# Products of two activations in whole fp32 instead of three products of split parts, in a kernel of two transformer blocks

## The chip, the cores and the metric

One core of a Trainium2 chip runs the whole kernel in one launch. The metric is the device time of an execution in microseconds (us); three executions took 1322.33, 1323.85 and 1326.26 us, the median is 1323.85. The execution that the profiler recorded took 1332.18 us, of which its span (first to last instruction) is 1330.4.

## The reference

Two blocks on 256 tokens of width 1024, all fp32. The first block: a mixer (gated causal convolution of 31 taps beside attention with 8 heads of 64 and a forget gate), attention of 4 heads of 128 over 256 memory rows, and an MLP with squared ReLU of width 4096. The second block puts 16 meta tokens ahead and runs a state space mixer (24 heads of 64 in 4 groups, state 128, chunks of 128 tokens) beside a short convolution, and then a layer of 16384 single-neuron experts:

```
q = (t @ w_q).reshape(T, 8, 2, 128)
s = einsum('thsd,hskd->thsk', q, sub_keys)          # scores against 2 x 128 sub keys
v_half, i_half = top_k(s, 16)                       # then the best 16 of 16 x 16 sums
experts = i1 * 128 + i2                             # 8 x 16 experts a token
act = gelu(einsum('td,tkd->tk', t, expert_u[experts])) * gates
out = einsum('tk,tkd->td', act, expert_v[experts])
```

A final norm gives the output (256 tokens without the meta tokens). The products of two activations are q with k, probabilities with v, the same two against the memory, in the state space mixer C with B, B with x, C with the state and the masked C-B scores with x; the sub key scores are a product of queries with a weight, but its two operands are treated in the same way.

## The kernel before, in words

Tokens lie in two tiles of 128. A weight comes from HBM in units of 128 x 1024 words, two units a transfer, on SyncE's queue. fp32 accuracy in matmuls is kept by splitting: ScalarE rounds an operand to fp32r (`hi`), VectorE or GpSimd subtracts to get the residual (`lo`), and `mm3` (L783) adds three products of fp32r parts, hi hi, hi lo and lo hi, into one PSUM bank. `unit` (L679) loads and splits a weight unit, `split` (L774) splits an activation that stands in PSUM or SBUF, `feat` (L821) multiplies a split weight with split activations (8 blocks of 128 rows, features on the partitions), `tok_unit` and `proj_out` do it with tokens on the partitions.

The products of two activations stand in `attend` (L1097: logits of two heads at a time, softmax, transposes, product with v), `recall` and `recalled` (L1247, L1261: the same against the memory), and in the loop over the four groups of the state space mixer (blocks bc, xt, state and y): B, C, x times dt, the decayed x, the states and the decay matrices times scores (`M`) are each split; `y` multiplies six heads with `M` hi against both halves of x (128 columns) and `M` lo against x hi (64 columns).

The expert layer: `to_n2` (L1603) normalizes, transposes and splits a token tile into `n2T`. `scores` (L1680) makes, for one head, two halves of queries (`feat` on `n2T` with split units of `w_q`), splits them, and multiplies them with split sub keys. Head 0 is done for one token tile at a time, so that its first routing can begin early; `route` is VectorE's top-16 search and index arithmetic. Its indices feed the indirect DMAs of GpSimd: 256 gathers (2 token tiles x 8 heads x 16), each bringing for 128 tokens a row of 2048 words (`expert_u` and `expert_v`), 1.049 MB. VectorE takes the dot product with the first half, ScalarE the GELU, and TensorE adds the second half into two banks, by diag(act) times 512 columns in whole fp32. Heads 1 to 7 have their scores made in the course of the first four heads' gathers. Ten units of `w_q` are loaded ahead into free k2 and act tiles (HELD), the rest come through raw tiles.

SBUF is given out in classes: k8 (tiles of 2048 words, 11 of them: at most 5 for `mid`, 2 `raw`, 4 split weights `w`, 2 split query weights `wq`, 10 gathered rows), act, k4 (1024 words, 4), k3, k2 and k1. PSUM has 2 banks `mm` and 6 `s`.

The order of the work is written by a planner (`Plan`): every operation is recorded with a cost and the tiles it uses, and a list scheduler gives each engine one fixed order; `SHIFTS` move the priority of each named block, `LATERS` say when GpSimd may take an operation that VectorE could do (`q.either`). On the chip each engine follows its list.

Of the kernel before, what the change touches and what calls it, by code (L numbers as in the profile page):

```python
# [33 lines left out]
QCONV = 2  # L34
MID, ROW = 5, 10
# [45 lines left out]
    "attend21.te": 199, "mo.gp": 1828, "state3.ve": -2216, "ln.gp": -447, "dt.sy": -536, "dt.sc": 1092,  # L81
# [107 lines left out]
SPAN = 3413.3  # L189
PIECE = 256  # L190
EARLY = {'s_kp': 3}
WINDOW = 3850
FIRST_MEM = 40
LEAD = 120
# [399 lines left out]
def trace(q, pool, psum, x, mem, meta, wts, sk, uv, cols, gains, ssdn, heads, out):  # L594
# [84 lines left out]
    def unit(k, w=UNIT, lead=None, at=None, place="k4"):  # L679
# [17 lines left out]
        if not lead:  # L697
            q.wait = q.place
# [72 lines left out]
    def sl(pr, *idx):  # L771
        return (pr[0][idx], pr[1][idx])
# [1141 lines left out]
```

## Time and profile before

| | |
|---|---|
| median of three executions | 1323.85 us (1322.33 to 1326.26) |
| profiled execution | 1332.18 us, span 1330.4 us, mean granted TensorE clock 0.975 |
| TensorE busy | 1142.5 us (86%), 5292 matmuls |
| VectorE busy | 956.9 us (72%) |
| ScalarE busy | 576.5 us (43%) |
| GpSimd busy | 494.0 us (37%) |
| DMA by GpSimd's queue | 268.45 MB, 48.8% of the 16 engines' span |
| DMA by SyncE's queue | 108.63 MB, 22.6% |

Every operation is issued by one helper, so the line is L548 throughout and groups are told apart by tiles: `k` stands for any tile of the k classes, `s` and `mm` for the PSUM banks, `s_...` for small tiles. A TensorE row counts instructions; a matmul in whole fp32 is two of them, one on fp32r parts is one. Mean times of matmuls hold the tail of the pipeline. In the slices of the page a digit is the busy share in tenths of a 40th of the span.

### The profile page before, as it was taken

Reading aid. Unit: us, or ns where it says so; the run is one execution under the profiler, and the core shown is the slowest. Engines: PE = TensorE matmul, PEld = TensorE weight load, DVE = VectorE, ACT = ScalarE, POOL = GpSimd, SP = SyncE. Lnnn points to the kernel's source line nnn. Section 1 sums busy time; section 2 is a strip of 40 time slices with the busy share of each in tenths; the row PEclk is TensorE's granted clock in tenths of the full one; section 3 lists DMA queues with packets and bytes.
Section 4 is the critical chain, followed back from the end, with each engine's and each line's share of the span. In section 5 each row is a group of like instructions: output and inputs, shape, how many; then the busy total and the mean of one; then the engine's idle time right before and its main releaser. Section 6 shows DMA issues by size and latency. Waiting matters only on the chain.

```text
span 1330.4 us, 16001 instructions
## 1 busy us (share of the span) xinstructions
PE 1142.5 (86%) x5292; PEld 788.3 (59%) x5292; DVE 956.9 (72%) x2210; ACT 576.5 (43%) x1162; POOL 494.0 (37%) x542
## 2 busy tenths in 40 slices
PE   6999889999998999999999997777778768777776
PEld 5988677999877998888865553332233223223222
DVE  7898877456557897885789999997555555555555
ACT  6647565445445965654354444323122122211221
POOL 4861250300001766431034464543434334343330
PEclk9999988999998999999999999999999999999998
DMA  7433333354554242446599999999999999999995
GB/s 278 150 119 139 146 120 134 128 221 159 197 217 158 100 150 107 161 157 224 190 344 409 410 421 422 421 421 421 422 420 422 421 421 422 421 421 422 422 421 208
DMA packets 55702, 378.09 MB, mean 284 GB/s; under 512 B 6322, under 2 KB 6962, under 8 KB 11460
## 3 DMA queue, kind: packets, MB, share of 16 engines
q0 software_dynamic: 36864, 268.45, 48.8%
q1 hardware_dynamic: 18756, 108.63, 22.6%
q8 instruction: 42, 0.69, 0.2%
q14 instruction: 40, 0.33, 0.1%
HBM read 376.01 MB, written 1.05 MB: 283 GB/s over the span
## 4 chain that ended last, share of the span: by engine, by line
PE 39%; DMA 34%; DVE 15%; issue 5%; ACT 3%; POOL 3%; another core or an unknown queue 0%; SPq 0%; POOLq 0%; DVEq 0%; ACTq 0%
DMA k<-in_uv,s_ei 32%; PE s L548 22%; PE mm L548 17%; DVE k L548 11%; ACT k L548 3%; DMA k<-in_wts 2%; POOL k L548 2%; DVE s_ix L548 1%; DVE s_v L548 1%; POOL act L548 1%; DMA k<-in_ssdn 1%; DMA x<-in_x 1%; DVE s_pos L548 0%; ACT L548 0%; DVE act L548 0%
## 5 line engine op out<-in xcount | busy, mean ns | idle before, releaser
L548 PE MATMUL s<-k,s_dg 128*128 128x512 f32 x1020 | 477.5, 614 | 129.1 <-ACT s_dg L548 128.6
L548 DVE SCALAR_TENSOR_TENSOR k<-k,k 128x1024 bf16<-128x1024 f32 x256 | 313.0, 1223 | 159.5 <-DMA k<-in_uv,s_ei 159.0
L548 PEld LDWEIGHTS s<-k,s_dg 128*128 128x128 f32 x1020 | 187.9, 193 | 400.3 <-ACT s_dg L548 206.6
L548 POOL DMA_INDIRECT k<-in_uv,s_ei x256 | 275.1, 1075 | 380.7 <-PE s L548 227.9
L548 PE MATMUL mm<-act,k 128*128 128x256 f32 (+4 forms) x2448 | 334.9, 289 | 9.0 <-DVE k L548 6.4
L548 PEld LDWEIGHTS mm<-act,k 128*128 128x128 f32 x2448 | 312.8, 191 | 25.0 <-DVE k L548 7.3
L548 ACT ACTIVATE k<-k 128x1024 fp32r<-128x1024 f32 (+11 forms) x293 | 231.3, 823 | 134.6 <-DVE k L548 58.1
L548 DVE TENSOR_TENSOR k<-k,k 128x1024 fp32r<-128x1024 f32 (+11 forms) x239 | 225.0, 970 | 51.7 <-ACT k L548 50.2
L548 POOL TENSOR_TENSOR k<-k,k 128x256 fp32r<-128x256 f32 (+2 forms) x205 | 160.7, 822 | 116.4 <-ACT k L548 100.2
L548 PE MATMUL s<-k,k 128*128 128x512 f32 (+8 forms) x868 | 191.5, 363 | 7.2 <-DVE k L548 3.6
L548 ACT ACTIVATE s_act<-s_dots,rx 128x2 f32<-128x2 f32 x129 | 38.1, 295 | 342.8 <-DVE k L548 342.7
L548 PEld LDWEIGHTS s<-k,k 128*128 128x128 f32 (+2 forms) x868 | 145.9, 191 | 37.2 <-ACT k L548 6.4
L548 ACT ACTIVATE s_dg<-ident,s_act 128x128 f32<-128x128 f32 x255 | 90.6, 394 | 87.4 <-DVE s_act L548 58.9
L548 PE MATMUL s<-k,act 128*128 128x512 f32 (+1 forms) x432 | 103.6, 385 | 1.8 <-ACT act L548 1.3
L548 PEld LDWEIGHTS s<-k,act 128*128 128x128 f32 x432 | 79.6, 194 | 13.8 <-ACT act L548 1.5
L548 ACT ACTIVATE k<-s 128x512 f32<-128x512 f32 (+10 forms) x99 | 46.9, 485 | 56.0 <-PE s L548 39.3
L548 ACT ACT_TABLE_LOAD x52 | 66.7, 1283 | 4.8 <-DVE k L548 2.1
L548 PE MATMUL s<-ident,k 128*128 128x128 f32 (+2 forms) x220 | 39.7, 308 | 30.0 <-DVE k L548 26.4
L548 DVE TENSOR_TENSOR k<-s,k 128x256 f32<-128x256 f32 (+8 forms) x100 | 44.8, 476 | 24.7 <-ACT k L548 15.2
L548 POOL TENSOR_TENSOR s_rstd<-s_ms,nhalf 128x1 f32<-128x1 f32 (+1 forms) x15 | 16.1, 1071 | 115.9 <-DVE s_ms L548 115.6
L548 POOL TENSOR_TENSOR s_r<-s_ms,nhalf 128x1 f32<-128x1 f32 x10 | 7.3, 732 | 127.4 <-DVE s_ms L548 124.0
L548 ACT ACTIVATE k<-mm 128x256 f32<-128x256 f32 (+3 forms) x70 | 25.9, 372 | 60.9 <-PE mm L548 53.3
(174 smaller groups left out, 776.5 us busy)
## 6 DMA issues: line engine op xcount, KB each, us to landing
k<-in_wts SPq DMA_DIRECT2D x89, 1024.0 KB, 4.8
k<-in_gains SPq DMA_DIRECT2D x9, 512.0 KB, 6.4
k<-in_uv,s_ei POOLq DMA_INDIRECT x256, 17.6
k<-in_wts SPq DMA_DIRECT2D x12, 256.0 KB, 7.0
act<-in_wts SPq DMA_DIRECT2D x4, 512.0 KB, 9.4
x<-in_x SPq DMA_DIRECT2D x2, 512.0 KB, 6.8
k<-in_mem SPq DMA_DIRECT2D x2, 512.0 KB, 6.1
k<-in_sk SPq DMA_DIRECT2D x2, 512.0 KB, 6.1
```

The source lines that it names most:

```text
L548: getattr(getattr(self.nc, e), method)(*a, **kw)
```

## The change

Products of two activations, the query projection and the sub key scores take whole fp32 operands, one product each. What made and held the split parts goes; query weights are used as they were loaded (`raw_unit`); `n2T` is one tile, copied half by ScalarE, half by VectorE. k8 has 12 tiles and up to 11 rows, the classes k3, `wq` and `s_kp` go, q and k of the attention share one k8 tile, as do the memory's keys and values, and v, the probabilities of the second token tile and the memory's q move to single k4 tiles. All values of `SHIFTS` and `LATERS` are others (left out here, as are repeated edits).

```diff
-QCONV = 2
-MID, ROW = 5, 10
+N8, MID, ROW = 12, 5, 11
-EARLY = {'s_kp': 3}
+EARLY = {}
...
+    def raw_unit():
+
+        q.shift -= QAHEAD
+        ts = loaded()
+        q.shift += QAHEAD
+        return [t[:, c:c + P] for t in ts for c in range(0, t.ap[-1][1], P)]
...
-            split(dst[0][:, c], dst[1][:, c], ps, scale=scale)
+            q.scalar.activation(dst[:, c], ps, AF.Copy, scale=scale)
...
-                mm3(ps[:, j], sl(qT, b, c0 + j, slice(i * P, i * P + P)),
-                    sl(kT, b, c0 + j, slice(0, kl)), False, j == 1)
+                q.tensor.matmul(ps[:, j], qT[b, c0 + j, i * P:i * P + P], kT[b, c0 + j, :kl],
+                                start=False, stop=j == 1)
...
-            split(PT[0][:, :, :, par], PT[1][:, :, :, par], tp)
+            q.scalar.activation(PT[:, :, :, par], tp, AF.Copy)
...
-            split(xdt[i][:, :, 0], xdt[i][:, :, 1], h6(t), eng=q.either)
+            q.vector.tensor_mul(h6(xdt[i]), h6(ps), hbc(dt3[:, 1 + i, hs]))
...
-        mm3(s1, sl(Bt, A_, 1), xdec, True, True)
+        q.tensor.matmul(s1, Bt[:, 1], xdec, start=True, stop=True)
...
-            M = pair(k4, 6, P)
-            split(M[0], M[1], E[i], eng=q.either)
...
-            mm3(yo, sl(CT, A_, slice(i * P, i * P + P)), pv[i], True, True)
+            q.tensor.matmul(yo, CT[:, i * P:i * P + P], pv[i], start=True, stop=True)
...
-            for h0, n in ((0, 4), (4, 2)):
-                yd = s_bank()[:, :n * P].rearrange("p (h j d) -> p h j d", h=n, j=2)
-                for h in range(n):
-                    q.tensor.matmul(yd[:, h], M[0][:, h0 + h], xdt[i][:, h0 + h], start=True, stop=False)
-                    q.tensor.matmul(yd[:, h, 0], M[1][:, h0 + h], xdt[i][:, h0 + h, 0], start=False, stop=True)
-                for j in range(2):
-                    to = h6(t)[:, h0:h0 + n]
-                    q.vector.tensor_add(to, yd[:, :, j], to)
+            yd = s_bank()[:, :GW]
+            for h in range(6):
+                q.tensor.matmul(h6(yd)[:, h], E[i][:, h], h6(xdt[i])[:, h], start=True, stop=True)
+            q.vector.tensor_add(t, yd, t)
...
-    n2T = pair(act, KD, T)
+    n2T = act(KD, T, dt=F32)
...
-        transposed(n2T, n2[i], i * P, P)
+        for c in range(0, KD, 4):
+            v = s_bank().rearrange("p (c t) -> p c t", c=4)
+            for j in range(4):
+                q.tensor.transpose(v[:, j], n2[i][:, (c + j) * P:(c + j + 1) * P], ident)
+            if c:
+                q.vector.tensor_copy(n2T[:, c:c + 4, i * P:i * P + P], v)
+            else:
+                q.scalar.activation(n2T[:, c:c + 4, i * P:i * P + P], v, AF.Copy)
...
-        kp = []
-        for c in (2 * h, 2 * h + 1):
-            kp.append(pair(lambda n, dt: small(n, "kp", dt), P))
-            split(kp[-1][0], kp[-1][1], skt[c // 8][:, c % 8])
...
-                ws[half] = ws.get(half) or unit(8, lead=0 if whole else None)
-                ps = feat(n2T, i0 * P, n * P, ws[half])
-                qp = pair(k1, n * P)
-                split(qp[0], qp[1], ps)
+                ws[half] = ws.get(half) or raw_unit()
+                ps = mm_bank()[:, :n * P]
+                for k in range(KD):
+                    q.tensor.matmul(ps, ws[half][k], n2T[:, k, i0 * P:(i0 + n) * P], start=k == 0, stop=k == KD - 1)
+                qp = k1(n * P)
+                q.scalar.activation(qp, ps, AF.Copy)
+                c = 2 * h + half
                 for i in range(i0, i0 + n):
-                    mm3(sp_[:, i, half], sl(qp, A_, slice((i - i0) * P, (i - i0) * P + P)),
-                        kp[half], True, True)
+                    q.tensor.matmul(sp_[:, i, half], qp[:, (i - i0) * P:(i - i0) * P + P], skt[c // 8][:, c % 8],
+                                    start=True, stop=True)
```

## Rows read from the trace of the kernel before

**Rows 1.** The page: busy tenths of TensorE and the DMA engines, 40 slices.
```profile
PE   6999889999998999999999997777778768777776
...
DMA  7433333354554242446599999999999999999995
```

**Rows 2.** Busy time by stage: stretch, us, busy (instructions), clock, DMA.
```profile
740.00:1310.00 570.00, 441.37 (x1044) 184.99 (x1043) 382.06 (x1020) 158.39 (x408) 243.02 (x228) 0.98 1.01 421
...
416.00:620.00 204.00, 196.31 (x1304) 181.92 (x1303) 169.72 (x321) 135.23 (x222) 103.32 (x130) 0.98 0.41 145
220.00:400.00 180.00, 178.45 (x1107) 158.93 (x1105) 101.63 (x141) 89.96 (x143) 14.43 (x19) 1.00 0.50 182
```

**Rows 3.** Busy time in slices of 5 us after the first gather.
```profile
665.00:670.00 5.00, 4.60 (x39) 4.39 (x38) 4.25 (x16) 2.63 (x6) 3.78 (x5) 1.00 0.82 282
...
685.00:690.00 5.00, 5.00 (x18) 2.55 (x18) 5.00 (x21) 4.21 (x9) 1.57 (x2) 1.00 0.66 218
...
735.00:740.00 5.00, 5.00 (x24) 3.28 (x23) 5.00 (x26) 2.20 (x5) 2.12 (x2) 1.00 0.96 351
```

**Rows 4.** Timeline of GpSimd, first gathers: start, us, what, [idle before, releaser].
```profile
663.95 1.17 POOL L548 DMA_INDIRECT k<-in_uv,s_ei  x1 [20.29 <-DVE s_gr L548]
...
670.61 1.20 POOL L548 DMA_INDIRECT k<-in_uv,s_ei  x1 [0.30 <-issue]
...
682.46 0.94 POOL L548 DMA_INDIRECT k<-in_uv,s_ei  x1 [6.70 <-PE mm L548]
687.68 1.08 POOL L548 DMA_INDIRECT k<-in_uv,s_ei  x1 [4.29 <-PE s L548]
```

**Rows 5.** Timeline of all engines from the last projection to the first gather.
```profile
639.70 1.28 DVE L548 TENSOR_TENSOR act<-s,act 128x512 fp32r<-128x512 f32 x2
...
644.88 3.11 PE L548 MATMUL mm<-act,k 128*128 128x128 f32 x24
...
648.04 0.28 DVE L548 TENSOR_TENSOR k<-mm,k 128x128 fp32r<-128x128 f32 x1
...
656.66 2.48 DVE L548 TENSOR_TENSOR k<-k,k 128x512 fp32r<-128x512 f32 x4
...
661.29 0.68 DVE L548 TENSOR_TENSOR k<-k,k 128x512 fp32r<-128x512 f32 x1
...
661.89 0.42 DVE L548 TENSOR_TENSOR k<-mm,k 128x256 fp32r<-128x256 f32 x1
662.22 0.68 DVE L548 TENSOR_TENSOR k<-k,k 128x512 fp32r<-128x512 f32 x1
```

**Rows 6.** Timeline of TensorE, 676 to 702 us, dense runs.
```profile
682.93 1.64 PE L548 MATMUL mm<-act,k 128*128 128x256 f32 x12
...
689.37 7.13 PE L548 MATMUL s<-k,s_dg 128*128 128x512 f32 x16
```

**Rows 7.** Timeline of TensorE, 120 to 140 us, dense runs.
```profile
125.50 1.03 PE L548 MATMUL s<-k,inv 128*128 128x256 f32 x4
...
129.78 1.39 PE L548 MATMUL s<-inv,k 128*128 128x1 f32 x12
...
133.81 3.96 PE L548 MATMUL s<-k,k 128*128 128x512 f32 x16
```

**Rows 8.** Groups of TensorE by form, 416 to 620 us.
```profile
L548 PE MATMUL mm<-act,k 128*128 128x272 f32 x367 | 55.4, 293 | 0.6 <-DVE k L548 0.6
...
L548 PE MATMUL s<-a,trilr 16*16 16x24 f32 x2 | 0.2, 184 | 0.0
```

**Rows 9.** Groups of VectorE by form, 416 to 620 us.
```profile
L548 DVE TENSOR_TENSOR k<-k,k 128x384 fp32r<-128x384 f32 x12 | 8.0, 693 | 0.5 <-ACT k L548 0.5
...
L548 DVE TENSOR_TENSOR k<-k,k 128x768 fp32r<-128x768 f32 x6 | 6.1, 1036 | 0.0
```

**Rows 10.** Groups of ScalarE by form, 416 to 620 us.
```profile
L548 ACT ACTIVATE k<-k 128x384 fp32r<-128x384 f32 x20 | 10.0, 521 | 7.0 <-DVE k L548 5.5 <-PE s L548 1.4
```

**Rows 11.** Chain of waits after the first gather: start, us, what.
```profile
708.86 9.24 DMA k<-in_uv,s_ei
```

More of the change, by code (lines that the diff above doesn't have):

```diff
@@ L53 @@
 SHIFTS = {
[27 rows of a table removed]
-    "attend21.te": 199, "mo.gp": 1828, "state3.ve": -2216, "ln.gp": -447, "dt.sy": -536, "dt.sc": 1092,
[83 rows of a table removed]
-LATERS = {
[22 rows of a table removed]
[23 rows of a table added]
+    "mo.gp": 1535, "state3.ve": -1696, "ln.gp": -529, "dt.sy": -251, "dt.sc": 1399, "gate11.sc": -1087,
[84 rows of a table added]
+LATERS = {
[22 rows of a table added]
 SPAN = 3413.3
 PIECE = 256
-EARLY = {'s_kp': 3}
+EARLY = {}
 WINDOW = 3850
@@ L611, in cls @@
         return t.rearrange(pat, **dict(zip(names[:-1], dims[:-1])))
-    N8 = MID + RAW_BUFS + CONV_BUFS
     def k4(*dims, dt=F32):
@@ L677, in load_early, with loaded @@
         q.wait = None
+    def loaded(at=None):
+        if early:
+            return early.pop(0)
+        u = st["next"] if at is None else at
+        st["next"] += at is None
+        if u % 2:
+            return [second_half.pop(u)]
+        t = k8("raw", RAW_BUFS)
+        q.sync.dma_start(t, wts[u // 2])
+        second_half[u + 1] = t[:, UNIT:]
+        return [t[:, :UNIT]]
+    def raw_unit():
[3 more added lines that the diff above has]
+        return [t[:, c:c + P] for t in ts for c in range(0, t.ap[-1][1], P)]
     def unit(k, w=UNIT, lead=None, at=None, place="k4"):
-        ahead = AHEAD if lead is None else QAHEAD
+        ahead = AHEAD
         lead = LEAD if lead is None else lead
         q.shift -= ahead
-        if early:
-            ts = early.pop(0)
-        else:
-            u = st["next"] if at is None else at
-            if u % 2 == 0:
-                t = k8("raw", RAW_BUFS)
-                q.sync.dma_start(t, wts[u // 2])
-                second_half[u + 1] = t[:, UNIT:]
-                ts = [t[:, :UNIT]]
-            else:
-                ts = [second_half.pop(u)]
-            st["next"] += at is None
+        ts = loaded(at)
         q.shift += ahead - lead
-        if not lead:
-            q.wait = q.place
         if place == "k2":
@@ L705, in unit @@
             else:
-                kind = ("wq", QCONV) if not lead else ("w", CONV_BUFS)
-                hi, lo = halves(k8(*kind, F32R), UNIT)
+                hi, lo = halves(k8("w", CONV_BUFS, F32R), UNIT)
             n = UNIT // len(ts)
@@ L713, in unit @@
             q.scalar.activation(h, t, AF.Copy)
-            (q.either if lead else q.vector).tensor_sub(l, t, h.bitcast(F32))
-        q.wait = None
+            q.either.tensor_sub(l, t, h.bitcast(F32))
         q.shift += lead
@@ L1006, in gated @@
         q.vector.tensor_mul(ups[c][:, 30:], ap, sg)
-    qT = pair(k4, 4, T)
-    kT = pair(k4, 4, T)
+    qT, kT = two(4, T)
     def qk(c):
-        for dst, scale in ((qT, 0.125), (kT, None)):
+        for dst, scale in ((qT, 0.125), (kT, 1.0)):
             ps = feat(hT, 0, T)
-            split(dst[0][:, c], dst[1][:, c], ps, scale=scale)
+            q.scalar.activation(dst[:, c], ps, AF.Copy, scale=scale)
     q.block("gated0")
@@ L1083, in trace @@
     q.block("v")
-    vt = pair(k4, NT, 512)
+    vt = k4(NT, 512)
     vp = [s_bank() for i in range(NT)]
@@ L1088, in trace @@
     for i in range(NT):
-        split(vt[0][:, i], vt[1][:, i], vp[i])
+        q.scalar.activation(vt[:, i], vp[i], AF.Copy)
     q.block("qk2")
@@ L1100, in attend @@
         kl = nk * P
-        PT = pair(k4 if i else k2, nk, 2, 2, P)
+        PT = (k4 if i else k2)(nk, 2, 2, P)
         for par in range(2):
@@ L1126, in attend @@
             for k in range(nk):
-                mm3(ps[:, j], sl(vt, A_, k, slice(c * P, c * P + P)), sl(PT, A_, k, j),
-                    k == 0, k == nk - 1)
+                q.tensor.matmul(ps[:, j], vt[:, k, c * P:c * P + P], PT[:, k, j],
+                                start=k == 0, stop=k == nk - 1)
         for b in range(2):
@@ L1169, in trace @@
     q.block("mem")
-    mk = pair(k4, 4, T)
+    mk, mv = two(4, T)
+    mv = mv.rearrange("p a b -> p (a b)").rearrange("p (i n) -> p i n", i=NT)
     mT = pair(act, KD, T)
@@ L1233, in trace @@
         ps = feat(mT, 0, T)
-        split(mk[0][:, c], mk[1][:, c], ps)
+        q.scalar.activation(mk[:, c], ps, AF.Copy)
     q.wait = q.last()
@@ L1243, in trace @@
     q.wait = None
-    qT = pair(k4, 4, T)
+    qT = k4(4, T)
     moT = pair(k4, 4, T)
@@ L1250, in recall @@
         for i in range(NT):
-            mm3(ps[:, i], sl(qT, A_, h, slice(i * P, i * P + P)), sl(mk, A_, h), True, True)
+            q.tensor.matmul(ps[:, i], qT[:, h, i * P:i * P + P], mk[:, h], start=True, stop=True)
         e = softmax(ps, NT, T, scale=rsc)
@@ L1256, in recall @@
                 q.tensor.transpose(tp[:, k, i * P:i * P + P], e[:, i, k * P:(k + 1) * P], ident)
-        PT = pair(k2, 2, T)
-        split(PT[0], PT[1], tp)
+        PT = k2(2, T)
+        q.scalar.activation(PT, tp, AF.Copy)
         return PT
@@ L1263, in recalled @@
         for k in range(2):
-            mm3(ps, sl(mv, A_, k, slice(h * P, h * P + P)), sl(PT, A_, k), k == 0, k == 1)
+            q.tensor.matmul(ps, mv[:, k, h * P:h * P + P], PT[:, k], start=k == 0, stop=k == 1)
         split(moT[0][:, h], moT[1][:, h], ps)
@@ L1270, in trace @@
         ps = feat(hT, 0, T)
-        split(qT[0][:, c], qT[1][:, c], ps)
+        q.scalar.activation(qT[:, c], ps, AF.Copy)
         q.block(f"recall{c}")
@@ L1274, in trace @@
     q.block("mv")
-    mv = pair(k4, NT, 512)
     vp = [s_bank() for i in range(NT)]
@@ L1279, in trace @@
     for i in range(NT):
-        split(mv[0][:, i], mv[1][:, i], vp[i])
+        q.scalar.activation(mv[:, i], vp[i], AF.Copy)
     for c in range(4):
@@ L1458, in trace @@
         q.block(f"bc{g}")
-        BT = pair(k1, TM)
-        CT = pair(k1, T)
-        Bt = pair(k1, 2, P)
-        b = conv_silu(12 + g)
-        split(BT[0], BT[1], b)
-        c = conv_silu(16 + g, META - 4)
-        split(CT[0], CT[1], c[:, 4:])
+        BT = conv_silu(12 + g)
+        CT = conv_silu(16 + g, META - 4)[:, 4:]
+        Bt = k1(2, P)
         ps = s_bank()
-        q.tensor.transpose(ps[:META, :P], b[:, :META], ident)
-        q.tensor.transpose(ps[:, P:T], b[:, META:META + P], ident)
-        split(Bt[0][:META, 0], Bt[1][:META, 0], ps[:META, :P])
-        split(Bt[0][:, 1], Bt[1][:, 1], ps[:, P:T])
+        q.tensor.transpose(ps[:META, :P], BT[:, :META], ident)
+        q.tensor.transpose(ps[:, P:T], BT[:, META:META + P], ident)
+        q.scalar.activation(Bt[:META, 0], ps[:META, :P], AF.Copy)
+        q.scalar.activation(Bt[:, 1], ps[:, P:T], AF.Copy)
         q.block(f"decay{g}")
@@ L1498, in trace @@
         q.block(f"xt{g}")
-        xdt = [cls("k3", 768, 2, 6, 2, 64, dt=F32R) for _ in range(NT)]
-        xdec = pair(k2, GW)
-        xdm = pair(k2, GW)
+        xdt = [k2(GW) for _ in range(NT)]
+        xdec = k2(GW)
         Y = [k2(GW) for _ in range(NT)]
@@ L1508, in trace @@
                 q.tensor.transpose(ps[:, c * P:(c + 1) * P], xs[c][:, t0:t0 + P], ident)
-            t = k2(GW)
-            q.vector.tensor_mul(h6(t), h6(ps), hbc(dt3[:, 1 + i, hs]))
-            split(xdt[i][:, :, 0], xdt[i][:, :, 1], h6(t), eng=q.either)
+            q.vector.tensor_mul(h6(xdt[i]), h6(ps), hbc(dt3[:, 1 + i, hs]))
             q.vector.tensor_mul(h6(Y[i]), h6(ps), hbc(hb[:, 24 + 6 * g:30 + 6 * g]))
             if i == 0:
-                t2 = k2(GW)
-                q.either.tensor_mul(h6(t2), h6(t), hbc(dec[:, 1, hs]))
-                split(xdec[0], xdec[1], t2, eng=q.either)
+                q.either.tensor_mul(h6(xdec), h6(xdt[i]), hbc(dec[:, 1, hs]))
         ps = s_bank()[:META, :GW]
@@ L1519, in trace @@
             q.tensor.transpose(ps[:, c * P:(c + 1) * P], xs[c][:, :META], ident)
-        t = k2(GW)[:META]
-        q.vector.tensor_mul(h6(t), h6(ps), hbc(dd[:META, hs], META))
-        split(xdm[0][:META], xdm[1][:META], t)
+        xdm = k2(GW)[:META]
+        q.vector.tensor_mul(h6(xdm), h6(ps), hbc(dd[:META, hs], META))
         q.block(f"state{g}")
         s0 = s_bank()[:, :GW]
-        mm3(s0, sl(Bt, slice(0, META), 0), sl(xdm, slice(0, META)), True, True)
+        q.tensor.matmul(s0, Bt[:META, 0], xdm, start=True, stop=True)
         s1 = s_bank()[:, :GW]
-        mm3(s1, sl(Bt, A_, 1), xdec, True, True)
-        pv = [pair(k2, GW) for _ in range(NT)]
-        split(pv[0][0], pv[0][1], s0)
-        t = k2(GW)
-        q.vector.tensor_mul(h6(t), h6(s0), hbc(dec[:, 2, hs]))
-        q.vector.tensor_add(t, s1, t)
-        split(pv[1][0], pv[1][1], t, eng=q.either)
+        q.tensor.matmul(s1, Bt[:, 1], xdec, start=True, stop=True)
+        pv = [k2(GW) for _ in range(NT)]
+        q.scalar.activation(pv[0], s0, AF.Copy)
+        q.vector.tensor_mul(h6(pv[1]), h6(s0), hbc(dec[:, 2, hs]))
+        q.vector.tensor_add(pv[1], s1, pv[1])
         cb = s_bank()
         for i in range(NT):
-            mm3(cb[:, i * P:i * P + P], sl(BT, A_, slice(META + i * P, META + i * P + P)),
-                sl(CT, A_, slice(i * P, i * P + P)), True, True)
+            q.tensor.matmul(cb[:, i * P:i * P + P], BT[:, META + i * P:META + i * P + P],
+                            CT[:, i * P:i * P + P], start=True, stop=True)
         cbm = k1(NT, P)
@@ L1725, in trace @@
     st["next"] += HELD
-    q.place = q.last()
     q.block("experts")
```

261 rows, old and new, of tables (LATERS, SHIFTS) are left out of this document.

## The prediction

> **What bounds the kernel now.** I read the page first: its 40 slices show two halves. Up to about half of the span TensorE is at 9 tenths in most slices and the DMA engines at 2 to 5; after that DMA stands at 9 and TensorE at 7 [rows 1]. The busy time by stage gives the sizes [rows 2]: from 740 to 1310 us DMA is fully busy at 421 GB/s, in the MLP (220 to 400) TensorE is busy 178.5 of 180 us, in the state space stage (416 to 620) 196 of 204 with VectorE at 170 and ScalarE at 135. So the second half is a transfer: 256 gathers of 1.049 MB are 268.4 MB, at 421 GB/s 637.6 us. Nothing the change does makes those bytes fewer. What can move is the time of the first gather, the loss of bandwidth just after it, and the front that leads up to it.
>
> The first gather is issued at 663.95 [rows 4]. In slices of 5 us [rows 3] the rate is then 282 GB/s in the first, 218 in the fifth and still 351 in the fifteenth; the shortfalls against 421 of these 15 slices from 665 to 740 (those three shown) add to some 3.5 MB, 8.4 us of full rate. The gather queue shows why: six gathers leave one after the other (663.95 to 670.61), a seventh a little later, the eighth waits 6.7 us for a matmul into mm and the ninth 4.3 us for one into s [rows 4]. The code gives the number: the k8 class has 11 tiles, n2 holds one, the last two raw weight tiles two, the split query weights (kind wq) two, six are left for rows.
>
> **The change part by part.**
>
> *Price of a product.* Before, a product is three single instructions on fp32r parts; a whole fp32 product shows as two instructions (the 510 expert products as 1020). Dense runs: 12 fp32r instructions of 256 columns in 1.64 us less about 0.16 of tail, 0.123 each, 0.37 a product [rows 6]; 16 of 512 columns in 3.96, 0.238 each [rows 7]. Whole fp32: 16 of 512 columns in 7.13 us, 0.434 each, 0.87 a product [rows 6]. For 256 columns the only row is 4 in 1.03 us [rows 7]: 0.34 to 0.52 a product, depending on how much is tail; I take 0.43, half of the 512 price. For narrow ones, 12 of one column in 1.39 us less tail are 0.104 each [rows 7], 0.21 a product (bounds 0.18 to 0.30, the upper one being three narrow instructions, that is no gain). So 128 columns: three by 0.107 become 0.21, a gain of 0.11; 256: a loss of 0.06; 384 lies between 256 and 512: three by 0.18 become 0.65, a loss of 0.11 (ends: 0.43 to 0.87).
>
> The Trainium skill, FP8 and Floating Point Precision, section TensorE Precision Notes, puts a true fp32 product at four passes through the array where a reduced one is a single pass; by that alone each of these products would grow by a third, 0.37 to 0.49 at 256 columns. The trace agrees only for wide products and less than that (0.43 by the row), and goes the other way at 128; what the rule would make of the time is the third rival.
>
> *Attention and memory (to 220 us).* 28 products of 256 columns: 28 x 0.06 = +1.7; 8 of 128: -0.9. TensorE +0.8 us. Gone are the residual subtractions of q, k, v, probabilities and memory keys and values, on VectorE, each between two products. I take 3 us of shorter waiting, net -2 (ends: +4, with the upper price and no relief, to -6).
>
> *State space stage.* Per group four products of 384 (s0, s1, yo twice): 16 x 0.11 = +1.8. Eight of 128 (cb): -0.9. The 48 products of scores with inputs: an instruction of 128 and one of 64 columns become one product of 64, two instructions again: 0. Sum +0.9. VectorE loses at least the 12 subtractions of 384 and 6 of 768, 14.1 us [rows 9], besides adds and small ones; ScalarE the 20 rounding copies of 384, 10.0 us [rows 10]; both of M's halves, and a second PSUM bank, go too. How much of this shows? Pricing the 19 forms of matmul in this stretch (first 367 x 0.13, last two) as dense runs gives some 190 us [rows 8] against 204: 14 us in which TensorE waits or runs on half clock. VectorE at 83% is next to it and on the same chain. I take 6 of the 14 back, net -5 (ends: +0.9 to -13; at the upper price +5).
>
> *From the last projection to the first gather.* This chain is VectorE's and serial, 24 us from the second subtraction of n2T to the gather [rows 4, 5]. (a) n2T: two rounding copies on ScalarE, then two subtractions, 1.28 us from 639.70 [rows 5]; now one copy on each engine side by side: -1.1. (b) Query products on 128 columns: 24 instructions in 3.11 us [rows 5] become 16 by 0.107: -1.1 for each half, -2.2. (c) The residual of the queries, 0.28 us and its hand-over [rows 5], twice: -0.7. (d) Splitting the next query weights lies on VectorE between the steps of the first routing: 2.48 us at 656.66, 0.68 at 661.29 and 0.68 at 662.22, with a query residual of 0.42 between [rows 5]: -4.3. (e) Sub key splits in the same stretch, some 1.2. Sum -9.5. What is late next is the routing itself (top-16 searches and index arithmetic), which stays. Ends: -4, if (a) to (c) are covered by what else queues there, to -12.
>
> *After the first gather.* wq tiles are gone and k8 has 12: with n2 and two raw tiles nine rows instead of six, later eleven. At 2.49 us a gather and 9.2 us from issue to landing where none is ahead of it [rows 11], four in flight keep the engines full, so the eighth and ninth gather no longer wait for matmuls. Of the 8.4 us, the first slice's 1.7 is start-up and stays; I take 5 (ends 0 to 6.7). The splits of the other seven heads leave VectorE and ScalarE: 0, since the gathers cover that work; were VectorE and not DMA late there, it would be a gain on top.
>
> From 740 on: 0. The end (last gather to last store) is untouched.
>
> **Sum:** -2 - 5 - 9.5 - 5 = -21.5 us. The profiled execution took 1332.18 us (span 1330.4 and 1.8 around it), so 1310.7; it is 8.3 us, 0.6%, above the median of the three runs, 1323.85. Taken off the median: **1302 us**.
>
> **Rivals.**
>
> 1. *TensorE alone is the front's bound.* For: 178.5 of 180 in the MLP, 196 of 204 after it [rows 2]. Against: a sum of priced instructions that leaves 14 us. Then the relief of VectorE is hidden and the dearer products are paid: +0.8 + 0.9 - 9.5 - 5 = -12.8, 1311 us.
> 2. *The state space stage falls to TensorE's own time* and attention gains its best: -13 - 6 - 11 - 6 = -36, 1288 us. For: VectorE at 170 of 204. Against: chains through softmax and gates stay.
> 3. *Slower: TensorE becomes the bound of the score stage and starves the gathers.* In the first 145 us after the first gather there are 58 gathers of 4 x 0.434 = 1.74 us, 101 us, and seven heads: 16 query products and 4 narrow ones each, 16 x 0.43 + 4 x 0.21 = 7.7, together 155 us; 10 too much (before: 7.1 a head, 151). Nine rows less four in flight cover five gathers, 12 us. Above that it decides: at 0.52 a head is 9.2, the overrun 20, so 8 us of starved gathers; the gain after the first gather is lost; 256 columns in attention cost +4.2 and 384 at the 512 price +5.5, less 1.8 on narrow ones. -9.5 + 8 + 4.2 + 5.5 - 1.8 = +6.4, 1330 us. For: TensorE is at 5.00 of 5 us in many slices up to 740 [rows 3]. Against: the 512 price halves to 0.43, and the seven heads need not be done by 145 us.
>    By the four-pass rule named above (Trainium skill, FP8 and Floating Point Precision) a head would be 16 x 0.49 + 4 x 0.43 = 9.6 us, so this rival is that rule's case too.
> 4. *No change.* All start shifts are new; the freed places on VectorE and TensorE before the first gather are filled with the other token tile's work, and the gather still leaves at about 664: 0, 1324 us. Against: its chain loses instructions of its own, whatever stands between.
>
> **How the numbers follow.** Forecast 0.61 (its own range 1294 to 1310), rival 1 0.20, rival 2 0.07, rival 3 0.06, rival 4 0.06. About 0.3%, 4 us, is what a measurement of this kernel can tell from no change. Faster: 0.61 + 0.20 + 0.07 = 0.88; within 0.3%: 0.06; slower: 0.06. The range leaves out rivals 3 and 4 and the edge of 2: 1286 to 1318.
>
> **What would show it.** First gather at 644 to 652 us instead of 663.95, of which 9.5 between the last projection's matmuls and it; nine gathers without a wait for a matmul, and the rate at 420 within 10 us of the first; from there to the end of the span the same 660 us or less; the state space stage some 5 us shorter with VectorE under 75%. Query products of 256 columns at 0.43 us a pair. Wrong if pairs of 256 columns take 0.5 us, if TensorE is at 100% and DMA under 400 GB/s in the 100 us after the first gather, or if the first gather doesn't come earlier.

## The result, and the profile after

The changed kernel takes 1289.86 us (median of four runs, 1288.56 to 1292.05); the kernel before 1325.05 (1322.33 to 1328.81). The ratio is 0.9734, 95% interval 0.9705 to 0.9763: 35 us faster, where 21.5 were forecast. The time lies inside the range (1286 to 1318), but below the range of the likeliest case (1294 to 1310); only rival 2, with its 1288 and a chance of 0.07, stood there. Its profiled run took 1292.05 us with a span of 1290.3, 40.1 less than the span before; some 5 us of that is the profiled run of before, which lay 7 us above its median.

The page of the kernel after, the same slices of busy tenths as [rows 1], with VectorE:

```profile
PE   5999899999998999999999997877877777777776
...
DVE  7887767655657966965899999955555555554555
...
DMA  7444433554643344438699999999999999999995
```

DMA is at 9 from slice 21 on, as before, but a slice is shorter now: that is 645 us where it was 665. VectorE stands at 9 in the six slices 21 to 26, in which the other heads' scores and routings are made. Busy time in the state space stage, cut at the same distances from the MLP's first down projection and from the last norm (both below) as the 204 us of [rows 2], and in slices of 5 us after the first gather, as [rows 3]:

```profile
401.50:596.50 195.00, 191.89 (x1293) 175.88 (x1292) 145.63 (x273) 115.83 (x183) 78.51 (x96) 1.00 0.41 145
...
630.00:635.00 5.00, 5.00 (x22) 3.69 (x21) 4.35 (x26) 0.57 (x2) 3.78 (x5) 1.00 0.71 236
635.00:640.00 5.00, 5.00 (x29) 4.50 (x28) 4.28 (x15) 0.99 (x5) 4.08 (x4) 1.00 0.97 354
640.00:645.00 5.00, 5.00 (x22) 3.79 (x21) 4.97 (x25) 3.23 (x6) 2.23 (x2) 1.00 1.00 418
```

TensorE is busy 191.9 of 195 us there at full granted clock (196 of 204 at 0.98 before), VectorE at 75% instead of 83%. The rate stands at 418 GB/s in the slice from 640 us, ten after the first gather; before it was still 351 after 71. The timeline of GpSimd, which answers to [rows 4], has the last norm (`rx`) and the gathers:

```profile
615.72 0.92 POOL L544 TENSOR_TENSOR rx<-s_ms,nhalf 128x1 f32<-128x1 f32 x1 [20.43 <-DVE s_ms L544]
...
629.71 1.16 POOL L544 DMA_INDIRECT k<-in_uv,s_ei  x1 [4.37 <-DVE s_gr L544]
...
641.59 0.94 POOL L544 DMA_INDIRECT k<-in_uv,s_ei  x1 [0.30 <-issue]
645.71 1.15 POOL L544 DMA_INDIRECT k<-in_uv,s_ei  x1 [3.18 <-PE s L544]
```

The first gather leaves at 629.71, 34.2 us earlier. Nine go one after the other, the ninth at 641.59; the tenth waits 3.2 us. The timeline of TensorE, with the dense runs that [rows 5, 6] had of the old products:

```profile
618.36 1.95 PE L544 MATMUL mm<-act,k 128*128 128x128 f32 x16
...
639.71 3.62 PE L544 MATMUL mm<-act,k 128*128 128x256 f32 x16
```

Sixteen instructions of 256 columns are eight whole products: 3.62 us less 0.16 of tail is 0.216 an instruction, 0.43 a product.

For the rest of the text the kernel is cut at four events, read from the first start of a group or from GpSimd's timeline: the MLP's first up projection (`s<-act`, 512 columns), its first down projection (`s<-act,k`, 512 columns), the last norm `rx`, the first gather, and the end of the span. Groups of the kernel after: count, shortest, median and longest ns, first to last start:

```profile
L544 PE MATMUL s<-act x24: 387/394/795, 198.3 to 211.0; 128*128 128x512 f32 x24
...
L544 PE MATMUL s<-act,k x24: 388/393/399, 367.1 to 378.0; 128*128 128x512 f32 x24
```

All kernels by these cuts (us), with the median and its ratio to the kernel before on the same chip:

| kernel | start to MLP | down projection to `rx` | `rx` to first gather | gather to end | median | ratio, 95% |
|---|---|---|---|---|---|---|
| before | 211.2 | 257.6 | 24.8 | 666.4 | 1325.05 | 1 |
| after | 198.3 | 248.6 | 14.0 | 660.6 | 1289.86 | 0.9734 (0.9705 to 0.9763) |
| att_only | 208.7 | 254.7 | 24.8 | 665.1 | 1326.90 | 0.9994 (0.9977 to 1.001) |
| order_att | 231.9 | 257.7 | 24.7 | 666.0 | 1343.45 | 1.0099 (1.0068 to 1.0129) |
| att_shifts | 194.5 | 254.9 | 24.7 | 665.8 | 1311.48 | 0.9868 (0.9829 to 0.9907) |
| att_order_c0 | 194.4 | 254.9 | 24.7 | 665.6 | 1313.20 | 0.9887 (0.9858 to 0.9916) |
| att_ssm | 197.8 | 249.1 | 24.7 | 665.0 | 1308.70 | 0.9853 (0.9812 to 0.9894) |
| scores | 208.7 | 258.8 | 14.0 | 659.6 | 1312.00 | 0.9878 (0.9837 to 0.9919) |
| te_att | 209.5 | 249.9 | 14.0 | 660.2 | 1305.04 | 0.9841 (0.9807 to 0.9875) |
| vec_att | 227.5 | 249.4 | 14.0 | 660.1 | 1323.57 | 0.998 (0.9966 to 0.9994) |
| vec_plan | 233.9 | 248.3 | 14.0 | 661.4 | 1325.86 | 0.9975 (0.9957 to 0.9992) |
| vec_free | 228.0 | 249.0 | 14.0 | 660.8 | 1322.69 | 0.9964 (0.9945 to 0.9983) |
| vec_ssm | 195.6 | 278.1 | 14.0 | 660.1 | 1319.21 | 0.9942 (0.9924 to 0.9961) |
| vec_sco | 195.9 | 249.4 | 15.4 | 660.7 | 1292.45 | 0.9745 (0.9713 to 0.9777) |

The cuts come from one profiled execution of each kernel. That of order_att took 8.5 us more than its median, that of before 7, the others lie within 2.2 of theirs. Kernels with one and the same front differ in the first column by 2 to 3 us (198.3, 195.9, 195.6), so less than that is not read from it; the third column agrees within 0.1 us among kernels with the same score code. Of the 40.1 us of span 12.9 came before the MLP, 9.0 from the first down projection to `rx` (for short, the state space stage), 10.8 between `rx` and the gather, 5.8 after it, and the rest in the MLP.

### The profile page after: what moved, and what is told of

It is laid out like the page before. It is cut to its first block, busy times and chain, and to the rows that moved or that the text cites. A ratio compares the mean times of both kernels' runs of the same rounds, so it can differ in the third digit from the quotient of the medians.

```text
span 1290.3 us, 15247 instructions
## 1 busy us (share of the span) xinstructions
PE 1126.7 (87%) x5047; PEld 772.2 (60%) x5048; DVE 888.3 (69%) x2064; ACT 536.2 (42%) x1084; POOL 533.1 (41%) x529
## 4 chain that ended last, share of the span: by engine, by line
PE 40%; DMA 36%; DVE 13%; issue 6%; ACT 2%; POOL 2%; POOLq 0%; SPq 0%; DVEq 0%; ACTq 0%
DMA k<-in_uv,s_ei 35%; PE s L544 24%; PE mm L544 17%; DVE k L544 9%; ACT k L544 2%; POOL k L544 1%; DVE s_ix L544 1%; DMA x<-in_x 1%; ACT L544 1%; DVE s_v L544 1%; DVE s_pos L544 1%; DVE act L544 0%; DVE s_best L544 0%; POOL act L544 0%; DVE x L544 0%
## 5 line engine op out<-in xcount | busy, mean ns | idle before, releaser
L544 POOL DMA_INDIRECT k<-in_uv,s_ei x256 | 319.4, 1248 | 317.1 <-DMA k<-in_uv,s_ei 145.6
L544 PE MATMUL mm<-act,k 128*128 128x256 f32 (+4 forms) x2240 | 316.9, 296 | 2.7 <-DVE k L544 1.9
L544 PEld LDWEIGHTS mm<-act,k 128*128 128x128 f32 x2240 | 294.5, 192 | 16.8 <-issue 5.9
L544 ACT ACTIVATE k<-k 128x1024 fp32r<-128x1024 f32 (+7 forms) x239 | 199.5, 865 | 88.4 <-DVE k L544 37.8
L544 DVE TENSOR_TENSOR k<-k,k 128x1024 fp32r<-128x1024 f32 (+9 forms) x191 | 186.6, 1004 | 65.7 <-ACT k L544 59.3
L544 POOL TENSOR_TENSOR k<-k,k 128x256 fp32r<-128x256 f32 (+2 forms) x198 | 156.4, 826 | 118.5 <-ACT k L544 101.1
L544 PE MATMUL s<-k,k 128*128 128x512 f32 (+6 forms) x832 | 190.1, 371 | 1.6 <-ACT k L544 1.5
L544 ACT ACTIVATE k<-s 128x512 f32<-128x512 f32 (+8 forms) x99 | 46.5, 484 | 65.8 <-PE s L544 47.7
L544 ACT ACTIVATE k<-mm 128x256 f32<-128x256 f32 (+2 forms) x70 | 26.3, 376 | 70.9 <-PE mm L544 70.7
L544 PEld LDWEIGHTS s<-ident,k 128*128 128x128 f32 (+2 forms) x220 | 28.2, 152 | 34.3 <-DVE k L544 25.0
```

Source lines behind the costliest of these rows:

```text
L544: getattr(getattr(self.nc, e), method)(*a, **kw)
```

## The experiments

**Undoing and doing parts.** Theory: the terms add up, and the front's 13 us are VectorE's freed time. Rivals: the new start shifts gave it, or the shorter hand-over from engine to engine.

*att_only*: the attention and memory edits in the kernel before, old shifts.

```diff
-            split(PT[0][:, :, :, par], PT[1][:, :, :, par], tp)
+            q.scalar.activation(PT[:, :, :, par], tp, AF.Copy)
...
 SHIFTS, LATERS: as before
```

> The kernel before with the attention and memory edits alone (whole fp32 products, no residual subtractions), start shifts all as before; state space stage and scores as before. If freeing VectorE gave the front's gain: the first matmuls of the MLP start 8 to 13 us earlier than the 211 of before, 1312 to 1317 us. If the new start shifts gave it: 0 to -3, 1322 to 1325 us. The forecast's own term was -2: 1323.

Measured 1326.90, ratio 0.9994: nothing, and the MLP at 208.7, which is also where scores has it, whose front is that of before. VectorE was freed (156.4 us of work up to the MLP, 171.6 in before) and no time came of it.

*att_shifts*: the same with the changed kernel's shifts for the blocks up to the MLP.

```diff
 (att_only)
-    "forget": -8060, "start": -7252, ...
+    the changed kernel's values of SHIFTS and LATERS for these blocks
```

> As the one before it, but with the changed kernel's start shifts for the blocks up to the MLP. By either theory the front is now the changed kernel's: MLP from 196 to 200 us, -11 to -15, 1310 to 1314 us. The difference to the kernel without these shifts is what the shifts are worth in this stage: 0 to 4 us by the VectorE theory, 8 to 12 by the other.

1311.48: 0.9868, and the MLP at 194.5. With the edit in place the shifts are worth 14 us, more than either theory gave them. At 145 us the two kernels are still level, both in the same products (`s<-k,act`, 512 columns). Where the time goes after that, the timeline of TensorE in att_only shows; in brackets is the idle time before a row, and who ended it:

```profile
155.75 0.66 PE L548 MATMUL s<-ident,k 128*128 128x128 f32 x4 [3.67 <-DVE k L548]
160.29 1.94 PE L548 MATMUL s<-ident,k 128*128 128x128 f32 x8 [3.88 <-DVE k L548]
...
166.51 5.94 PE L548 MATMUL mm<-act,k 128*128 128x256 f32 x35 [2.68 <-DVE k L548]
...
206.19 1.29 PE L548 MATMUL s<-ident,k 128*128 128x128 f32 x8 [3.83 <-DVE k L548]
208.68 1.65 PE L548 MATMUL s<-act 128*128 128x512 f32 x3 [1.20 <-DVE act L548]
```

The same in att_shifts:

```profile
155.68 1.00 PE L540 MATMUL s<-ident,k 128*128 128x128 f32 x4 [4.31 <-DVE s_ms L540]
...
191.30 1.32 PE L540 MATMUL s<-ident,k 128*128 128x128 f32 x8 [0.44 <-DVE k L540]
194.49 0.97 PE L540 MATMUL s<-act 128*128 128x512 f32 x3 [1.88 <-DVE act L540]
```

The transposes behind `ident` at 155 us are those after the mixer's norm, the ones at 206 and 191 those after the memory's. At these seams TensorE waits for rows that VectorE normalizes: 10.2 us at the first in att_only and 5.0 at the second, 4.3 and 2.3 in att_shifts. Busy time of att_only, a slice of 10 us behind the waits and the whole stretch to its MLP (the columns as in [rows 2]; the first busy time is TensorE's, the first of the last three numbers its mean granted clock),

```profile
160.00:170.00 10.00, 6.86 (x28) 6.06 (x29) 9.93 (x16) 3.36 (x6) 4.88 (x6) 0.50 0.30 105
...
150.00:208.70 58.70, 40.48 (x222) 33.97 (x221) 40.35 (x66) 32.44 (x65) 23.82 (x29) 0.87 0.36 125
```

and of att_shifts to its own:

```profile
150.00:194.50 44.50, 36.72 (x217) 31.66 (x217) 34.83 (x59) 30.02 (x60) 23.74 (x27) 0.96 0.44 162
```

For nearly the same instructions (222 and 217) TensorE is busy 3.8 us longer in att_only, at a mean granted clock of 0.87 instead of 0.96, and idle for 18.2 us instead of 7.8. Together that is the 14.2 us by which the MLP starts earlier.

*order_att*: is it the order alone? The code of before with those shifts, all but the first block's, with which the planner finds an order for this code; and *att_order_c0*, the edits with the same table.

```diff
 order_att: code as before
 att_order_c0: code as att_only
-    old values of SHIFTS and LATERS, 41 blocks up to the MLP
+    the changed kernel's values; "conv0" keeps its old ones
```

> The code of the kernel before, residual subtractions and three part products and all, with the changed kernel's start shifts for the 41 of 42 blocks up to the MLP (the first, conv0, keeps its old one). If the new order gives the front's gain by itself: the first matmuls of the MLP start at 195 to 199 us instead of 209 to 211, -12 to -15, 1310 to 1313 us. If the order pays only on the VectorE time that the edit frees: 208 us or later, 1322 to 1335.

> The control to that: the same start shifts with the attention and memory edits. If the conv0 block's shift doesn't matter, this is the kernel with all 42 again: MLP from 194 to 199 us, 1309 to 1313 us. If it does: 205 to 209, 1322 to 1327, and the run of the old code with these shifts says nothing on the order.

The control keeps the gain (1313.20, 0.9887). The old code with the new shifts is slower than before: 1343.45, ratio 1.0099, beyond the worse of its two expectations, and the MLP at 231.9 (in a profile that took 8.5 us more than the median). TensorE's rows in order_att, and the group of the first up projection:

```profile
136.90 1.22 PE L539 MATMUL s<-k,k 128*128 128x512 f32 x2 [5.85 <-ACT k L539]
140.82 12.76 PE L539 MATMUL s<-k,k 128*128 128x512 f32 x46 [2.70 <-DVE k L539]
...
180.14 2.22 PE L539 MATMUL s<-ident,k 128*128 128x128 f32 x8 [4.17 <-DVE k L539]
```

```profile
L539 PE MATMUL s<-act x24: 387/396/793, 231.9 to 241.7; 128*128 128x512 f32 x24
```

It loses its time ahead of the stretch in which att_shifts gains: the last transposes of the first seam start at 180.1 us, those of att_only at 160.3. So the edit alone gives 0, the new shifts alone cost 13 us, and both together give 15 to 17.5 (the two kernels' ratios). Neither the first theory nor its rival stands: the gain belongs to the pair. Two limits: one set of shifts was tried on the old code, so no run shows that it has no better order; and the edit does not only free VectorE, it also halves the tiles of q, k, v and the probabilities. Which of the two lets the shifts pay was not tested.

*att_ssm*: attention, memory and state space edits with the changed kernel's shifts up to the last projection, the scores as before. *scores*: the score edits alone, with the changed kernel's shifts for the score and expert blocks.

```diff
 att_ssm: att_shifts, and
-        mm3(s1, sl(Bt, A_, 1), xdec, True, True)
+        q.tensor.matmul(s1, Bt[:, 1], xdec, start=True, stop=True)
...
 scores: kernel before, and
-N8 = MID + RAW_BUFS + CONV_BUFS
+N8, MID, ROW = 11, 5, 10
-                ws[half] = ws.get(half) or unit(8, lead=0 if whole else None)
+                ws[half] = ws.get(half) or raw_unit()
```

> The changed kernel without the score edits: attention, memory and the state space stage by whole products with the changed kernel's start shifts up to the last projection; scores, their weights and their shifts as before. If the stages add: -13 -2 -9 of the front, 1325 - 24 = 1301 us (1298 to 1305), the stretch from the last norm to the first gather stays at 24 to 25 us, and six gathers leave without a wait.

> The kernel before with the score edits alone (ten places for rows, eleven of the class, in place of eleven and twelve), the changed kernel's start shifts for the score and expert blocks. If the stages add: the front as before, from the last norm to the first gather 14 us instead of 24.75, and 5 to 6 us of the bandwidth loss gone: 1325 - 16 = 1309 us (1306 to 1312). If the chain's gain needed the freed engines of the earlier stages: 1314 to 1320.

att_ssm is at 1308.70, 4 us outside its expectation. Its state space stage takes 249.1 us against 254.9 of att_shifts: the stage's own edit (with its shifts) is worth 6, not the 9 between the two profiles. The medians bear out only 2 of it, since the front of att_ssm ends 3.3 us later than that of att_shifts, about what equal fronts differ by. The other 3 us were there as soon as the attention edits were: in that stretch before, scores and order_att have one wait of 1.5 to 1.9 us of TensorE for VectorE's `s_ms`, which the kernels with the attention edit don't have; why, no run here shows. scores is at 1312.00, the edge of its range: 14.0 us from `rx` to the gather and 659.6 after it, both as in the kernel after, with one place for rows fewer; so the places that the split query weights gave up are enough, and the twelfth tile adds nothing that shows. The two ratios multiplied, 0.9853 x 0.9878 = 0.973, are the whole change's 0.9734: nothing is left over that the intervals (0.004 on each side) could show. In the state space stage and the scores edit and shifts were always changed together, so what each gives there alone, as in the front, is open.

**Putting time back.** The other way round: does the changed kernel have room on VectorE, or on TensorE?

*te_att*: each product of attention and memory twice.

```diff
+    def doubled(ps, w, h, start, stop):
+        q.tensor.matmul(ps, w, h, start=start, stop=start)
...
+        q.tensor.matmul(ps, w, h, start=start, stop=stop)
...
-            q.tensor.matmul(ps[:, i], qT[:, h, i * P:i * P + P], mk[:, h], start=True, stop=True)
+            doubled(ps[:, i], qT[:, h, i * P:i * P + P], mk[:, h], True, True)
```

> The changed kernel with every product of attention and memory (28 of 256 columns, 8 of 128) issued twice on TensorE, so some sums count double: 28 x 0.525 + 8 x 0.21 = 16 us more of TensorE before the MLP. If TensorE sets the pace of the front: +13 to +16, 1303 to 1306 us. If VectorE and the chains between engines set it, so that TensorE has room: +2 to +6, 1292 to 1296. Were it +0 the price of the whole fp32 products would not matter at all.

1305.04, ratio 0.9841, that is 0.0107 x 1325 = 14 us more, and the MLP at 209.5, 11 to 14 later. Up to the MLP TensorE is busy for 188.1 us instead of 175.4, 12.7 more, so its time in the front counts nearly in full. Dearer products would have been paid for.

*vec_att*: VectorE subtractions behind the copies, results unused. The helper that issues them is written out in this cut and the later ones; the planner counts them as taking no time, except in vec_plan.

```diff
             q.scalar.activation(PT[:, :, :, par], tp, AF.Copy)
+            q.vector.tensor_sub(waste, tp, PT[:, :, :, par])
```

> The changed kernel, with one VectorE subtraction put back behind each copy of q, k, v, the probabilities and the memory keys, queries and values (some 36 of 256 to 512 elements, about 14 us of VectorE up to the MLP); its result is thrown away, so the products wait for the copy alone as before. The order tables stay. Theory A (the front before the MLP gained because VectorE was freed): most of it comes back, 1290 + 8 to 13 = 1298 to 1303 us, and the first matmuls of the MLP start at 206 to 211 us instead of 198. Theory B (the products wait for one engine fewer, a shorter chain): VectorE's time itself is covered, at most +3 us, 1290 to 1293. Theory C (the new order tables gave it): also at most +3.

1323.57: all but 3 us of the whole change's gain is gone, 33 us for 16.65 us of VectorE, and 20 beyond the range of theory A. The MLP starts at 227.5, 29 later. TensorE's waits up to the MLP (what waits for what: us in total, times, the longest) and its busy time there, in vec_att,

```profile
PE s L544 <- DVE k L544: 31.0, 9, 12.6
PE s L544 <- ACT k L544: 5.2, 8, 2.0
PE mm L544 <- DVE waste L544: 2.3, 3, 1.2
...
0.00:227.50 227.50, 183.85 (x1084) 157.51 (x1084) 173.54 (x351) 126.92 (x248) 97.83 (x127) 0.92 0.41 148
```

and in the kernel after:

```profile
PE s L544 <- DVE k L544: 15.6, 4, 12.7
...
PE s L544 <- ACT k L544: 1.8, 3, 1.3
...
0.00:198.30 198.30, 175.38 (x1079) 153.82 (x1080) 150.63 (x314) 126.22 (x247) 109.27 (x147) 0.98 0.47 166
```

The 12.6 is the first norm, in both. Few matmuls wait for the subtractions themselves; what comes late are the tiles that VectorE makes behind them (15 us more), and TensorE's idle time grows from 22.9 to 43.7 us. The other 8.5 us are busy time: the same work takes 183.9 instead of 175.4, at a mean granted clock of 0.92 against 0.98. On VectorE's side the view of the subtractions says what it waited for before them (us, times):

```profile
its engine sat idle before it (us, times) until:
  ACT k L544: 8.6, 7
```

So they took 16.65 us of its time and held it another 8.6 at the head of its queue, until ScalarE's copy was there.

*vec_plan* counts each subtraction in the planner, *vec_free* takes a constant as its source, so that it waits for nothing.

```diff
 vec_plan: planner's cost of the subtraction, ns
-        q.ops[-1].engs = [("vector", 0)]
+        q.ops[-1].engs = [("vector", 600)]
...
 vec_free:
-        q.vector.tensor_sub(w, src, dst)
+        q.vector.tensor_sub(w, z, z)        # z: ident, broadcast
```

> The first of the experiments again (32 subtractions behind the copies), but the order is drawn up with 0.6 us of VectorE counted for each, where there they were counted at nothing. If the 29 us came from an order that did not know of them: half or less, +5 to +14, 1295 to 1304 us. If VectorE has no time left there in any order: +20 to +33, 1310 to 1323 us.

> The changed kernel with the same 32 VectorE subtractions in the same places of its queue as in the first of the experiments, but over a constant, so that they wait for no copy and hold no bank; some 13 to 17 us of VectorE. That one took 29 us in the stretch up to the MLP. If it was VectorE's time: +13 to +29, 1303 to 1320 us, MLP from 209 to 226. If it was the waits for ScalarE's copies at the head of VectorE's queue: at most +8, 1298, MLP before 206.

vec_plan is no better (1325.86, 3 us beyond its worse expectation): an order that counts them, drawn up from the same shifts, hides nothing. vec_free (1322.69) missed its aim. VectorE's timeline:

```profile
4.43 1.42 DVE L544 TENSOR_TENSOR waste<-ident 128x512 bf16<-128x512 f32 x2
9.51 16.40 DVE L544 TENSOR_TENSOR waste<-ident 128x256 bf16<-128x256 f32 x30
```

Without a source to wait for, the planner put all 32 at the start, where VectorE makes the first norm. TensorE's wait for that norm grew from 12.7 to 28.7 us, 16 of the 30 that it lost. So it doesn't separate VectorE's time from its waits for copies at the head of its queue; how much of vec_att's 29 us is due to the 8.6 us of such waits is open.

*vec_ssm* and *vec_sco* do as vec_att does, in the state space stage and between the last projection and the first gather.

```diff
 vec_ssm:
             q.vector.tensor_mul(h6(xdt[i]), h6(ps), hbc(dt3[:, 1 + i, hs]))
+            q.vector.tensor_sub(waste, xdt[i], xdt[i])
...
 vec_sco:
                 q.scalar.activation(qp, ps, AF.Copy)
+                q.vector.tensor_sub(waste, qp, ps)
```

> The changed kernel with VectorE subtractions put back in the state space stage behind B, C, their transposes, the scaled inputs, the two states and the two masked score tiles (16 a group, some 5.5 us of VectorE a group, 22 us in all), results thrown away, and nothing waits for them but VectorE's own queue. If relief of VectorE gave the stage's 9 us: +7 to +11, 1297 to 1301 us. If the shorter chains gave it or TensorE binds there (191 of 194 us busy): at most +3, 1293.

> The changed kernel with VectorE subtractions put back between the last projection and the first gather only: over the transposed n2, over the queries of the first head and over its two raw weight units, results thrown away (about 5 us of VectorE, in the chain to the first gather). The prediction takes that chain to be VectorE's and serial: the first gather then leaves 4 to 5 us later (634 instead of 630) and the time is 1294 to 1295 us. If the 10.8 us came from the order or from TensorE, it is 1290 to 1291.

vec_ssm: VectorE's busy time on these alone (52 of them; 22 us were planned), and TensorE's waits from 400 to 643 us:

```profile
400.00:643.00 243.00, 29.61 (x52) 0.94 0.42 154
...
PE s L544 <- DVE k L544: 9.2, 7, 3.4
PE mm L544 <- DVE k L544: 6.8, 5, 3.0
...
365.20:643.30 278.10, 254.43 (x1519) 224.41 (x1518) 204.09 (x374) 137.54 (x220) 90.50 (x100) 0.93 0.41 152
```

The last row has TensorE's busy time, first after the stretch's length, from the first down projection to `rx`; the same in the kernel after:

```profile
367.10:615.70 248.60, 239.06 (x1519) 214.69 (x1518) 178.48 (x322) 136.63 (x220) 82.51 (x100) 0.99 0.45 163
```

29.6 us of VectorE make the stage 29.5 longer, where +11 was expected at the most, though VectorE is at 75% in it. Of the 29.5 TensorE is idle for 14.1 (23.7 against 9.5); the other 15.4 are the same 1519 instructions taking longer, at a mean granted clock of 0.93 against 0.99. The way back is no mirror image: the change took 24 us of work off VectorE in this stage (169.7 to 145.6) and gained 9. vec_sco, the group of its subtractions:

```profile
L544 DVE TENSOR_TENSOR waste<-k x4: 689/692/693, 603.5 to 605.7; 128x512 bf16<-128x512 f32 x4
L544 DVE TENSOR_TENSOR waste<-s,act x4: 673/676/685, 613.3 to 624.5; 128x512 bf16<-128x512 f32 x4
L544 DVE TENSOR_TENSOR waste<-mm,k x4: 273/288/292, 616.3 to 629.1; 128x128 bf16<-128x128 f32 x4
```

Those over the raw weights ran at 603 to 606, ahead of the chain that they were meant for. The eight others, 3.9 us for both token tiles, half of it for the first, made `rx` to gather 15.4 instead of 14.0. That bears out a serial chain; the size is smaller than expected because the dose in it was. The time, 1292.45, lies between the two expectations and can't be told from that of the kernel after by its interval, so the reading rests on the cut alone.

## Why the prediction was right in sign and too small

*Price of a product.* Right: 0.43 at 256 columns, half of the price at 512, is what the dense run shows. The groups of 28 products in attention and memory, before and after:

```profile
L548 PE MATMUL s<-k,k 128*128 128x256 f32 x84 | 14.8, 311 | 2.6 <-ACT k L548 2.6
...
L544 PE MATMUL s<-k,k 128*128 128x256 f32 x56 | 14.7, 387 | 0.0
```

They take the same time, tails included, so even the +1.7 is not seen. The count leaves out eight products of q and k (64 rows, 256 columns), another +0.5 at its price; they took 4.2 us before and 3.7 after. At 128 columns 0.107 an instruction was too low on both sides: 24 fp32r instructions took 3.11 us [rows 5], 16 whole ones 1.95. The Trainium skill, FP8 and Floating Point Precision, section TensorE Precision Notes, counts four passes for a true fp32 product; the trace comes near it at 256 columns, 0.43 against 0.123 for one fp32r instruction [rows 6], 3.5 times, and not at 128, where the 16 instructions in 1.95 us are eight products of 0.24 against 0.13 for one fp32r instruction [rows 5], less than twice. By the rule the third rival's price would have come; by the rows it didn't.

*Attention and memory: the term that failed.* Forecast -2 (ends +4 to -6), measured -13 in the profiles and -15 to -17.5 by the two kernels with the pair, which hold the 3 us of the next stage too. The step put the gain down to three us of shorter waiting and costed the start shifts at nothing; the runs show that the edit under its old shifts gives nothing that can be measured, and that the new shifts, which cost 13 us in the old code, give the whole with it. Shifts appeared only in rival 4, as a way to lose.

*State space stage.* Forecast -5, measured -9, of which -6 is the stage's own. The bound of 14 us of waiting and half clock was sound: 3 us of waits are left of it, at clock 1.00. Calling VectorE with its 83% "next to TensorE" and taking 6 of the 14 back was too mild: vec_ssm shows that work put on VectorE there comes out in full at the end, half of it as longer busy time of TensorE at a lower clock.

*Last projection to first gather.* Forecast -9.5, measured -10.8 in every kernel with the score edits (vec_sco, with its subtractions, apart) and 0 in every one without. The chain is VectorE's and serial, as written; whether the score edits give this under the old shifts, no run shows. One step is off: part (b) is -1.2 to -1.4 a half by its own prices, not -1.1; the rows give 3.11 and 1.95 us, -1.2.

*After the first gather.* Forecast -5, measured -5.8; nine gathers without a wait, as written, and 418 GB/s in the slice that begins ten us after the first. scores, with 659.6, shows that ten places for rows do as well as eleven.

*The rivals.* Rival 1's premise holds in the front (te_att) and even so its number fails, since the products' price didn't show and, together with the shifts, the relief of VectorE was not hidden. Rival 2, given 0.07, is nearest with its 1288 us, but by another split: it has -13 in the state space stage, where -9 was measured, and -6 in attention, where it was -13. That the time fell inside the range at all is owed to the end that this rival gave it, and so in part to luck. Rival 3 fails at the rate of 418 GB/s; rival 4 at the first gather, 629.71, earlier even than the 644 to 652 that were to show the forecast right.

## What to carry to other kernels

Where each engine follows one fixed order, work taken off an engine and an order drawn up for the lighter load can be one change: price them together, and test an edit under its own order before calling it worthless. A busy share says little of room: VectorE at 75% beside TensorE at 98% had none here. Put a known amount of work back on an engine and look how much comes out at the end. Cut the span at a few events and compare each stretch over all kernels; stretches that move alike in kernels with one edit in common point to that edit, or to what was always changed with it.

## What the runs showed of the hardware

A wait on TensorE cost more than its length: in att_only it waits 3.7 and 3.9 us between 152 and 160 us and 2.7 more before 166.5, and from 160 to 170 the granted clock is 0.50, the lower of its two levels (1.2 GHz), though it is busy for 6.9 of these 10 us. In vec_att and vec_ssm 21 and 14 us more of idle time came with 8.5 and 15.4 us more of busy time for the same work, at a lower mean clock.

A whole fp32 instruction of 256 columns has half the price of one of 512, 0.216 against 0.434 us [rows 6]; one of 128 columns has about a quarter, 0.112 (16 in 1.95 us, less 0.16 of tail). An instruction on fp32r parts is no cheaper at 128 columns than at 256: 24 of 128 columns take 3.11 us [rows 5], and so do 24 of 256 in order_att, below. So three of them cost more against one whole product at 128 columns than at 256.

```profile
71.54 3.11 PE L539 MATMUL mm<-act,k 128*128 128x256 f32 x24 [0.64 <-DVE k L539]
```
